# TensorE sums the gathered V rows of a mixture of experts, four tokens abreast, for two of three tiles

## The chip, the core and the metric

One Trainium2 chip, one core. The metric is the device time of one launch in microseconds (us), the median of several executions. Engines go by the names of the profile: PE is TensorE, PEld its weight loads, DVE is VectorE, ACT is ScalarE, POOL is GpSimd, SP is SyncE (it issues most DMAs); SPq, PEq and so on are their instruction queues. POOL issues the indirect (gathering) DMAs.

## The reference, cut to what matters

Two layers of a diffusion trunk over 512 latent tokens and, in layer 0, 256 context tokens of width 1024. Each layer mixes tokens (attention, a long convolution, a state space scan) and then runs a feed-forward net of 16384 experts, of which each token takes 128 (8 heads of 16):

```python
def peer_ffn(x, wq, sub_keys, u_tab, v_tab):
    ...
        best, pos = lax.top_k(cand, PEER_TOPK)
        expert = jnp.take_along_axis(cand_id, pos, axis=-1)
        gate = jax.nn.softmax(best, axis=-1)
        act = jax.nn.gelu(jnp.einsum('btd,bthkd->bthk', xc, u_tab[expert]).astype(jnp.float32))
        w = (gate * act).astype(xc.dtype)
        return jnp.einsum('bthk,bthkd->btd', w, v_tab[expert])
```

So a token's result is a sum of 128 rows of the V table, each of 1024 float32, with 128 weights. The change is in how this last sum is made for some tokens.

## The kernel before

The tokens stand in tiles of 128. There are six expert tiles to compute in layer 0 (four latent, two of context) and four in layer 1. They are computed in two ways.

*Dense* (`peer_u`, `peer_v`; four tiles in layer 0, three in layer 1): all 16384 experts for every token. `peer_u` goes through 128 chunks of the U table: DMA of 512 KB, a split into a high and a low half (ACT line 176, DVE line 160, since a product of float32 accuracy is made of three matmuls, `mm3`), 24 matmuls into the PSUM tile `pu` (layer 0, 512 columns) or `pm` (layer 1, 384 columns), GELU, and a store. `peer_v` goes through 128 steps of the V table: DMA of 512 KB (`x`, two buffers), the same split (`xh`, `xl`), the activations `va` times a gate table `gt` (loaded every eight steps), a split of that (`vwh`, `vwl`) and matmuls into accumulators `pa` that stay in PSUM for the whole loop: 24 per step in layer 0, 18 in layer 1. The gate tables come from `peer_table` (one-hot matrices `ohA`, `ohB` on DVE, matmuls into `ps`). Where the tables are done before all chunks of `peer_u` are, the chunks left over are computed inside `peer_v` ("fused" steps, into PSUM tiles `px`). In layer 1 there are such steps.

*Gathered* (`peer_gather`, lines 1191 to 1214; the two context tiles of layer 0 and one latent tile of layer 1): for each of the 128 experts of a token, one indirect DMA brings one row per token, so that a tile `gx` of 128 partitions (tokens) by 1024 floats holds the k-th expert of every token. The U phase takes 128 such tiles and DVE multiplies and sums each (line 1196). Then come GELU and the gate, and the V phase takes 128 tiles more; DVE multiplies each by the token's weight and adds it to the result (line 170, called from `add`). `gx` has four buffers: an indirect DMA waits until the tile four before it has been used.

The order of the work comes from `weave` (line 100): generators yield an estimated time and the one that is behind goes next. The framework then puts the instructions of each engine in one fixed order, by data dependencies and its own estimate of time; on the chip every engine goes through its list in order. Here the gather generator is woven with the others in three stretches: with `peer_u` and the table work (line 1531, line 1583), and then with `peer_v` (lines 1537, 1589). PSUM has eight banks. In layer 0's `peer_u` they are lent out as `m` (4), `u` (2), `s` (2); in its `peer_v` as `a` (7) and `x` (1); in layer 1 as `m` (4), `s` (2) and then `a` (6), `x` (2). `x` is needed by the fused steps.

Of the kernel before, what the change touches and what calls it, by code (L numbers as in the profile page):

```python
# [22 lines left out]
D = 1024  # L23
# [10 lines left out]
NCAND = OFFS[8] + 8  # L34
NE = 128 * 128
WAIT = -1

PV_NORM = 0
PV_GATEB = PV_NORM + NL * 2 * 8
# [7 lines left out]
class Trunk:  # L47
# [124 lines left out]
    def act(self, out, x, f, **k):  # L172
        self.nc.scalar.activation(out=out, in_=x, func=f, **k)  # L173
# [1000 lines left out]
            for x in hn:  # L1174
                self.tt(x, x, b, op)

    def gathered(self, pool, src, ids, use):

        lag, made = 1, []
        for k in range(128 + lag):  # L1180
            if k < 128:
                g = self.t(pool, [128, D], tag="gx", bufs=4)
                self.nc.gpsimd.indirect_dma_start(out=g, out_offset=None, in_=src,  # L1183
                                                  in_offset=bass.IndirectOffsetOnAxis(ap=ids[:, k:k + 1], axis=0))
                made.append(g)
            if k >= lag:
                with self.tc.issue_after(self.paced) if self.paced else nullcontext():
                    use(k - lag, made.pop(0))
            yield 1.6

    def peer_gather(self, pool, l, j, x, p, ids, dot, src, put):

        w = p[:, 2].rearrange("p h k -> p (h k)")

        def product(c, g):
            self.nc.vector.tensor_tensor_reduce(out=g, in0=g, in1=x, scale=1.0, scalar=0.0, op0=OP.mult, op1=OP.add,  # L1196
                                                accum_out=dot[:, c:c + 1])

        def add(c, g):
            if c:  # L1200
                self.stt(x, g, w[:, c:c + 1], x, OP.mult, OP.add)
            else:
                self.ts(x, g, w[:, 0:1], OP.mult)

        yield from self.gathered(pool, self.a["peer_un"], ids, product)
        self.act(dot, dot, AF.Gelu_apprx_tanh)
        self.tt(w, w, dot, OP.mult)
        yield from self.gathered(pool, self.a["peer_v"].rearrange("l e d -> (l e) d"), ids, add)
        y = self.t(pool, [128, D], tag="gx", bufs=4)
        self.nc.sync.dma_start(y, src)  # L1210
        self.tt(x, x, self.rows(pool, l, j, 5, "gx", 4), OP.mult)
        self.tt(x, x, y, OP.add)
        put(x)
        yield 4.0
# [20 lines left out]
    def peer_v(self, l, pool, h, act, G, xs, put, j):  # L1235
# [31 lines left out]
        for s in range(128):  # L1267
            i = order[s]
            if s % 8 == 0:
                gt = self.t(pool, [128, n, 8, 8, 16], tag="gt", bufs=2)  # L1270
                for q in range(n):
                    nc.sync.dma_start(gt[:, q], G[q][:, :, i:i + 8, :].rearrange("b p e t -> p b e t"))
            v = self.weights(vr[:, i:i + 1, :], None, pool, "x", 2)
            if s == 0:
                yield 0.0
            a = self.t(pool, [128, T], tag="va", bufs=2)
            if s < fused:
                u, u0 = activations(s + 1), u
                p = self.bank("x")[:, 0:T]
                for k in range(8):  # L1280
                    self.mm3(p, (u0[0][:, k], u0[1][:, k]), (h[0][:, k], h[1][:, k]), k == 0, k == 7)
                self.act(a, p, AF.Gelu_apprx_tanh)
            else:
                nc.sync.dma_start(a, act(i))
            if len(held) == 2 or held and s < 127:
                b = held.pop(0)
                for k in halves:
                    half(b, k)
            y = gt[:, :, :, i % 8, :]
            self.tt(y, a.rearrange("p (q b t) -> p q b t", q=n, b=8), y, OP.mult)  # L1290
            w = [self.t(pool, [128, n * 8, 16], F32R, tag=t, bufs=2) for t in ("vwh", "vwl")]
            with self.tc.issue_after(self.freed) if odd and 0 < s < fused else nullcontext():
                self.split(y.rearrange("p q b t -> p (q b) t"), *w)
            self.paced = self.cut.ins
            held.append((s, [z.rearrange("p b t -> p (b t)") for z in w], v))
            yield n * (2.6 if s < fused else 1.3)
        g2 = self.rows(pool, l, j, 5, "x", 2)
        for q in range(n):
            for b in held:
                for c in range(2):  # L1300
                    half(b, (q, c))
            x = self.t(self.wp, [128, D], tag="w", bufs=3)
            nc.sync.dma_start(x, xs[q])
            for c in range(2):
                k = slice(c * 512, c * 512 + 512)
                y = self.t(pool, [128, 512], tag="vy", bufs=2)
                z = acc[q, c]
                if (q, c) == odd and fused:
                    if fused < 128:
                        self.tt(part, part, z, OP.add)  # L1310
                    z = part
                self.tt(y, z, g2[:, k], OP.mult)
                self.tt(x[:, k], x[:, k], y, OP.add)
            put(q, x)
            yield 2.0

# [101 lines left out]
    def run(self):  # L1418
# [27 lines left out]
        def chain(*gens):  # L1446
            for g in gens:
                yield from g
# [69 lines left out]
        def gather():  # L1518
            for q in range(2):
                yield from until(("ids", q), "gx")  # L1520
                yield from self.peer_gather(C["gx"], 0, 1, *C[q], c1[q], lambda x: nc.sync.dma_start(c2[q], x))
            self.done.add("c2")

        side, gather = aside(), gather()
        with self.pool("ha") as ha:
            hs.append(self.halves(ha, TL))
            with self.psum(m=4, u=2, s=2), self.pool("ua") as ua:
                weave((chain(self.ctx_rest(0, xc, c1, vec[0, 0], st[0]), mark("c1"), ctx_side()), lambda: 1.1 if "c1" in self.done else 1.0, "m"),
                      (chain(until("h"), self.peer_u(0, ua, hs[0], TL, lambda i: act[i], "tabs"), mark("u")), lambda: 1.2 if "c1" in self.done else 10.0, "u"),
                      (part(side, "tables"), lambda: 1.25 if "c1" in self.done else 1.23 if "pg" in self.done else 0.8, "s"),  # L1530
                      (self.while_(gather, "tabs"), 1.69, "s"), (mods(1, range(6), 0, 1), 1.26, "m"))
            self.done.add(("mods", 1))
            with self.pool("pv", True) as pv:
                vl = self.peer_v(0, pv, hs[0], lambda i: act[i], G, x1, self.store(x2), 0)
                next(vl)
                with self.psum(a=7, x=1):
                    weave((vl, 1.0, "m"), (gather, 1.5, "s"))
# [20 lines left out]
        def gather():  # L1558
            for q in range(o):
                yield from until(("ids", 1, q))  # L1560
                yield from self.peer_gather(pg, 1, 0, hn[q], pk[q], ids[q], dot[q], x1[q], lambda x: final(q, x))

        gather = gather()
        pu = self.psum(m=4, s=2)
# [152 lines left out]
```

## Time and profile before

| | |
|---|---|
| median of 3 runs | 5661.28 us (5646.26 to 5666.2) |
| profiled execution | 5662.23 us; its span 5660.2 us |
| PE busy | 4899.3 us, 87% |
| PEld busy | 4022.5 us, 71% |
| DVE busy | 3729.2 us, 66% |
| ACT busy | 1758.3 us, 31% |
| POOL busy | 1426.1 us, 25% |
| DMA | 1333.38 MB, mean 236 GB/s |

The profile follows one execution. Its stretches, in time: token mixing of layer 0 until some 1740 us, with `peer_u` of layer 0 begun; the gathers of layer 0 begin at 1743 us; `peer_u` ends at 2543 us and `peer_v` runs until some 3400 us; token mixing of layer 1 until 4150 us; `peer_u` of layer 1 with tables until 4950 us; `peer_v` until the end. How to read it: busy shares over the whole span mix all these, so each stretch is looked at by itself. "DMA share" is the mean busy share of the core's 16 DMA engines (it can read slightly over 1), "PEclk" the granted clock of TensorE as a part of 2.4 GHz.

### The profile page before, as it was taken

Reading aid. Unit: us, or ns where it says so; the run is one execution under the profiler, and the core shown is the slowest. Engines: PE = TensorE matmul, PEld = TensorE weight load, DVE = VectorE, ACT = ScalarE, POOL = GpSimd, SP = SyncE. Lnnn points to the kernel's source line nnn. Section 1 sums busy time; section 2 is a strip of 40 time slices with the busy share of each in tenths; the row PEclk is TensorE's granted clock in tenths of the full one; section 3 lists DMA queues with packets and bytes.
Section 4 is the critical chain, followed back from the end, with each engine's and each line's share of the span. In section 5 each row is a group of like instructions: output and inputs, shape, how many; then the busy total and the mean of one; then the engine's idle time right before and its main releaser. Section 6 shows DMA issues by size and latency. Waiting matters only on the chain.

```text
span 5660.2 us, 72445 instructions
## 1 busy us (share of the span) xinstructions
PE 4899.3 (87%) x25801; PEld 4022.5 (71%) x25801; DVE 3729.2 (66%) x7594; ACT 1758.3 (31%) x2651; POOL 1426.1 (25%) x1626
## 2 busy tenths in 40 slices
PE   6798978869997888998888887998889588899898
PEld 5676657648885777786666676875678587798687
DVE  5643436644499899987676775534435989788755
ACT  3222423314432322332222223333233133333233
POOL 0003500000002343433444440405000322254400
PEclk7899989889998999999998998998999899999999
DMA  6557335666556888899999986561545777799975
GB/s 207 190 185 263 106 117 183 201 205 185 176 179 207 306 291 314 319 325 343 319 317 311 320 307 205 166 224 58 157 157 168 242 252 243 256 338 333 333 239 176
DMA packets 641793, 1333.38 MB, mean 236 GB/s; under 512 B 56437, under 2 KB 342390, under 8 KB 626328
## 3 DMA queue, kind: packets, MB, share of 16 engines
q1 hardware_dynamic: 522776, 871.53, 47.1%
q0 software_dynamic: 118656, 457.23, 23.0%
q8 instruction: 203, 3.33, 0.2%
q14 instruction: 158, 1.29, 0.1%
HBM read 1147.01 MB, written 181.49 MB: 235 GB/s over the span
## 4 chain that ended last, share of the span: by engine, by line
PE 27%; DVE 12%; DMA 11%; issue 10%; POOL 4%; ACT 1%; SPq 1%; POOLq 0%; DVEq 0%; ACTq 0%
PE pa L181 9%; PE two L181 4%; PE ps L181 4%; PE pu L181 3%; POOL gx L1183 3%; PE px L181 2%; DMA va<-t 2%; PE pf L181 2%; DMA gx<-in_peer_v_dram,t 2%; DVE t L170 2%; DVE wl L160 2%; PE pm L181 2%; DMA gx<-in_peer_un_dram,t 1%; DVE gx L1196 1%; DMA t<-ge 1%
## 5 line engine op out<-in xcount | busy, mean ns | idle before, releaser
L176 ACT CAST wh<-w 128x1024 fp32r<-128x1024 f32 (+1 forms) x550 | 545.9, 993 | 1611.2 <-PE pu L181 395.3
L160 DVE TENSOR_TENSOR wl<-w,wh 128x1024 fp32r<-128x1024 f32 (+1 forms) x550 | 639.4, 1164 | 555.4 <-ACT wh L176 545.3
L1183 POOL DMA_INDIRECT gx<-in_peer_un_dram,t x384 | 527.9, 1375 | 1501.1 <-DVE t L1196 691.6
L181 PE MATMUL pa<-xl,vwh 128*128 128x512 f32 x1664 | 673.1, 405 | 124.1 <-DVE xl L160 123.7
L1183 POOL DMA_INDIRECT gx<-in_peer_v_dram,t x384 | 543.6, 1416 | 680.1 <-DVE t L170 579.9
L181 PE MATMUL pa<-xh,vwh 128*128 128x512 f32 x1664 | 665.8, 401 | 28.1 <-ACT xh L176 21.4
L181 PE MATMUL pu<-t,wh 128*128 128x512 f32 x2048 | 659.0, 403 | 28.5 <-ACT ua L173 20.7
L181 PE MATMUL pa<-xh,vwl 128*128 128x512 f32 x1664 | 665.1, 400 | 1.2 <-DVE ss L167 1.1
L181 PE MATMUL pm<-t,wh 128*128 128x384 f32 (+1 forms) x2432 | 586.0, 328 | 59.1 <-ACT wh L176 54.4
L170 DVE SCALAR_TENSOR_TENSOR t<-gx,t,t 128x1024 f32<-128x1024 f32 x381 | 488.4, 1282 | 35.2 <-DMA gx<-in_peer_v_dram,t 33.3
L1196 DVE CUSTOM_DVE_ANT_0 gx<-gx,t 128x1024 f32<-128x1024 f32 x384 | 465.3, 1220 | 57.8 <-DMA gx<-in_peer_un_dram,t 57.4
L181 PEld LDWEIGHTS pm<-t,wh 128*128 128x128 f32 x2432 | 431.1, 196 | 77.7 <-ACT wh L176 72.2
L181 PEld LDWEIGHTS pa<-xl,vwh 128*128 128x128 f32 x1664 | 323.0, 194 | 213.2 <-DVE xl L160 147.0
L181 PEld LDWEIGHTS pu<-t,wh 128*128 128x128 f32 x2048 | 389.6, 194 | 111.6 <-ACT ua L173 26.8
L181 PE MATMUL pu<-t,wl 128*128 128x512 f32 x1024 | 412.9, 404 | 60.4 <-DVE wl L160 60.4
L181 PE MATMUL pm<-t,wl 128*128 128x384 f32 (+1 forms) x1216 | 396.9, 329 | 49.1 <-DVE wl L160 49.0
L181 PEld LDWEIGHTS pa<-xh,vwh 128*128 128x128 f32 x1664 | 322.0, 194 | 103.6 <-ACT xh L176 27.7
L176 ACT CAST vwh<-gt 128x512 fp32r<-128x512 f32 (+1 forms) x256 | 145.3, 568 | 794.9 <-PE pa L181 671.2
L181 PEld LDWEIGHTS pa<-xh,vwl 128*128 128x128 f32 x1664 | 323.5, 194 | 70.8 <-DVE vwl L160 3.5
L176 ACT CAST xh<-x 128x1024 fp32r<-128x1024 f32 x256 | 268.2, 1048 | 252.4 <-DMA x<-in_peer_v_dram 208.0
L160 DVE TENSOR_TENSOR xl<-x,xh 128x1024 fp32r<-128x1024 f32 x256 | 312.7, 1221 | 26.2 <-ACT xh L176 25.8
L160 DVE TENSOR_TENSOR gt<-va,gt 128x512 f32<-128x512 f32 (+1 forms) x256 | 156.6, 622 | 262.2 <-DMA va<-t 107.9
(371 smaller groups left out, 9154.3 us busy)
## 6 DMA issues: line engine op xcount, KB each, us to landing
w<-in_peer_u_dram SPq DMA_DIRECT2D x256, 512.0 KB
x<-in_peer_v_dram SPq DMA_DIRECT2D x256, 512.0 KB
w<-in_in_w_dram SPq DMA_DIRECT2D x128, 512.0 KB
t<-ge SPq DMA_DIRECT2D x56, 1024.0 KB
gt<-t SPq DMA_DIRECT2D x112, 512.0 KB
w<-in_mod_w_dram SPq DMA_DIRECT2D x96, 512.0 KB
dft<-in_dft_dram POOLq DMA_DIRECT2D x32, 1024.0 KB, 6.8
t<-ua SPq DMA_DIRECT2D x128, 256.0 KB
```

Source lines behind the costliest of these rows:

```text
L160: return (e or self.nc.vector).tensor_tensor(out=out, in0=a, in1=b, op=op)
L170: self.nc.vector.scalar_tensor_tensor(out=out, in0=a, scalar=s, in1=b, op0=op0, op1=op1)
L176: self.nc.scalar.copy(h, x)
L181: self.nc.tensor.matmul(out, l, r, start=start, stop=stop)
L1183: self.nc.gpsimd.indirect_dma_start(out=g, out_offset=None, in_=src, in_offset=bass.IndirectOffsetOnAxis(ap=ids[:, k:k + 1], axis=0))
L1196: self.nc.vector.tensor_tensor_reduce(out=g, in0=g, in1=x, scale=1.0, scalar=0.0, op0=OP.mult, op1=OP.add, accum_out=dot[:, c:c + 1])
```

## The change

For the first context tile of layer 0 and for the gathered tile of layer 1 the V phase is done by TensorE (new function `summed`). The indices and weights are transposed, so that one indirect DMA now brings the 128 rows of *one token* onto 128 partitions. A matmul with the 128 weights as one column among 32 (the others zero) as its stationary operand sums them. Four tokens, whose columns are in the four groups of 32 columns of the array, make a group: eight matmuls of 512 columns, four into each of two PSUM accumulators, 32 groups in all. The accumulators are taken from lane `m` in layer 0 and from `x` in layer 1; so the phase waits until the modulation matmuls (`("mods", 1)`) or the fused steps (`("fused", 1)`) are done. The second context tile keeps DVE. The buffers of `gx` become 7 in layer 0 and 8 in layer 1, for all gathers; in `peer_v` the tile `vy` is dropped (its product is written in place).

```diff
-    def gathered(self, pool, src, ids, use):
+    def gathered(self, pool, l, src, ids, use):
...
-                g = self.t(pool, [128, D], tag="gx", bufs=4)
+                g = self.t(pool, [128, D], tag="gx", bufs=GX[l])     # GX = [7, 8]
...
+    def summed(self, pool, l, src, ids, w, lane):
+        nc = self.nc
+        p = self.bank(lane)
+        f = self.t(pool, [128, 128], tag="gi", bufs=1)
+        nc.vector.tensor_copy(f, ids)
+        nc.tensor.transpose(p[:, 0:128], f, self.ident)
+        nc.tensor.transpose(p[:, 128:256], w, self.ident)
+        it = self.t(pool, [128, 128], I32, tag="git", bufs=1)
+        nc.vector.tensor_copy(it, p[:, 0:128])
+        wt = self.t(pool, [128, 4, 32], tag="gi", bufs=1)
+        nc.vector.tensor_copy(wt.rearrange("p g s -> p (g s)"), p[:, 128:256])
+        acc = [self.bank(lane) for _ in range(2)]
+        lag, made = GX[l] - 4, []
+        for n in range(128 + lag):
+            if n < 128:
+                t = 32 * (n % 4) + n // 4
+                g = self.t(pool, [128, D], tag="gx", bufs=GX[l])
+                nc.gpsimd.indirect_dma_start(out=g, out_offset=None, in_=src,
+                                             in_offset=bass.IndirectOffsetOnAxis(ap=it[:, t:t + 1], axis=0))
+                made.append(g)
+            if n % 4 == (lag - 1) % 4:
+                s = (n - lag - 3) // 4
+                if s >= 0:
+                    if s % 4 == 0:
+                        z = self.t(pool, [128, 4, 4, 32], tag="gz", bufs=2)
+                        nc.vector.memset(z, 0.0)
+                        nc.vector.tensor_copy(z.rearrange("p g s c -> p g (s c)")[:, :, s:s + 100:33], wt[:, :, s:s + 4])
+                    rows = [made.pop(0) for _ in range(4)]
+                    for c in range(2):
+                        for q in range(4):
+                            self.mm(acc[c][32 * q:32 * q + 32, :], z[:, q, s % 4, :], rows[q][:, c * 512:(c + 1) * 512], s == 0, s == 31)
+                yield 6.4
+        return acc
...
+        if lane:
+            yield from self.until(*[key] * (key is not None))
+            acc = yield from self.summed(pool, l, rows, ids, w, lane)
+        else:
+            yield from self.gathered(pool, l, rows, ids, add)
...
-                yield from self.peer_gather(C["gx"], 0, 1, *C[q], c1[q], lambda x: nc.sync.dma_start(c2[q], x))
+                yield from self.peer_gather(C["gx"], 0, 1, *C[q], c1[q], lambda x: nc.sync.dma_start(c2[q], x),
+                                            None if q else "m", ("mods", 1))
...
-                yield from self.peer_gather(pg, 1, 0, hn[q], pk[q], ids[q], dot[q], x1[q], lambda x: final(q, x))
+                yield from self.peer_gather(pg, 1, 0, hn[q], pk[q], ids[q], dot[q], x1[q], lambda x: final(q, x), "x", ("fused", 1))
```

Three places in the program's order (no times are in it). The first is TensorE's list in layer 0 where `peer_u` (`pu`) ends and `peer_v` (`pa`) begins, of the kernel before:

```order
L181 MATMUL pu_21586<-t_7724,wh_21581 128x512
L181 MATMUL pu_21586<-t_7723,wl_21582 128x512
L181 MATMUL pu_21586<-t_7723,wh_21581 128x512
L181 MATMUL pu_21586<-t_7724,wh_21581 128x512
L181 MATMUL pu_21586<-t_7723,wl_21582 128x512
L181 MATMUL pa_21658<-xh_21626,vwh_21637 128x512
L181 MATMUL pa_21662<-xh_21626,vwh_21637 128x512
```

And of the change, the last rows of 56 that stand there between the last `pu` and the first `pa` (`gx` is a token's gathered rows, `gz` the weight columns, `pm` the two accumulators):

```order
L182 MATMUL pm_18681<-gx_22199,gz_22017 32x512
L182 MATMUL pm_18682<-gx_22199,gz_22017 32x512
L182 MATMUL pm_18681<-gx_22201,gz_22017 32x512
L182 MATMUL pm_18682<-gx_22201,gz_22017 32x512
L182 MATMUL pm_18681<-gx_22203,gz_22017 32x512
L182 MATMUL pm_18682<-gx_22203,gz_22017 32x512
L182 MATMUL pm_18681<-gx_22287,gz_22017 32x512
L182 MATMUL pm_18682<-gx_22287,gz_22017 32x512
L182 MATMUL pa_21792<-xh_21753,vwh_21764 128x512
L182 MATMUL pa_21792<-xl_21754,vwh_21764 128x512
```

What moved: between the last `pu` and the first `pa` there was nothing; now the last seven of the 32 groups (28 tokens) stand there, since `peer_v` needs the PSUM banks that they accumulate in. The other 25 groups stand between chunks of `pu`, most of them two chunks apart, six of them one chunk. The second place is TensorE's list there, one such group among the chunks, of the change (`ps` is table work):

```order
L182 MATMUL ps_20107<-ohB_20054,ohA_20053 128x128 x4
L182 MATMUL pm_18681<-gx_19991,gz_20121 32x512
L182 MATMUL pm_18681<-gx_19993,gz_20121 32x512
L182 MATMUL pm_18681<-gx_19995,gz_20121 32x512
L182 MATMUL pm_18681<-gx_20113,gz_20121 32x512
L182 MATMUL pm_18682<-gx_19991,gz_20121 32x512
L182 MATMUL pm_18682<-gx_19993,gz_20121 32x512
L182 MATMUL pm_18682<-gx_19995,gz_20121 32x512
L182 MATMUL pm_18682<-gx_20113,gz_20121 32x512
L182 MATMUL ps_20139<-ohB_20101,ohA_20100 128x128 x4
```

What moved: DVE's four operations on four tiles `gx` became these eight matmuls. The third place is the start of layer 1's V phase. Before, on DVE, it began in a fused step of `peer_v` (`wl` and `w` are the U table's chunk of such a step):

```order
L160 TENSOR_TENSOR t_33412<-t_33412,t_33414 128x128
L165 TENSOR_SCALAR t_33411<-gx_40446,t_33412 128x1024
L160 TENSOR_TENSOR wl_40606<-w_40604,wh_40605 128x1024
L160 TENSOR_TENSOR gt_39956<-va_40457,gt_39956 128x24x16
L160 TENSOR_TENSOR vwl_40510<-gt_39956,vwh_40509 128x384
L170 SCALAR_TENSOR_TENSOR t_33411<-gx_40448,t_33412,t_33411 128x1024
```

Now it begins on TensorE after 34 of the 128 steps of `peer_v`, all fused steps being done (`px` are the accumulators):

```order
L182 MATMUL pa_40236<-xh_42214,vwl_42241 128x512
L182 MATMUL px_42203<-gx_42205,gz_42283 32x512
L182 MATMUL px_42203<-gx_42207,gz_42283 32x512
L182 MATMUL px_42203<-gx_42209,gz_42283 32x512
L182 MATMUL px_42203<-gx_42211,gz_42283 32x512
L182 MATMUL px_42204<-gx_42205,gz_42283 32x512
L182 MATMUL px_42204<-gx_42207,gz_42283 32x512
L182 MATMUL px_42204<-gx_42209,gz_42283 32x512
L182 MATMUL px_42204<-gx_42211,gz_42283 32x512
L182 MATMUL pa_40216<-xh_42245,vwh_42271 128x512
```

What moved: the 32 groups stand over 82 steps of `peer_v` that have no U chunk, two or three steps apart, and 12 steps follow the last; before, the V phase of this tile began at the fourth step.

## Rows read from the trace of the kernel before

**Rows 1.** Busy us by stretch: PE, PEld, DVE, ACT, POOL; PEclk; DMA share; GB/s.

```profile
1740.00:2180.00 440.00, 364.28 (x1747) 302.12 (x1746) 400.49 (x1090) 120.09 (x177) 177.19 (x132) 0.92 0.83 290
2180.00:2543.00 363.00, 339.53 (x1713) 286.61 (x1712) 325.98 (x699) 111.86 (x166) 144.04 (x103) 0.98 0.88 314
2549.00:2640.00 91.00, 82.71 (x333) 65.63 (x333) 72.37 (x82) 22.34 (x28) 35.45 (x27) 0.94 1.01 350
2640.00:3400.00 760.00, 646.82 (x2667) 519.12 (x2667) 550.75 (x698) 177.51 (x223) 337.54 (x242) 0.91 0.92 316
4350.00:4950.00 600.00, 470.05 (x2690) 448.04 (x2689) 519.40 (x1482) 180.63 (x271) 154.61 (x112) 0.90 0.72 247
4950.00:5200.00 250.00, 249.61 (x1264) 226.35 (x1263) 212.39 (x236) 87.56 (x120) 134.68 (x93) 1.00 0.93 334
5200.00:5400.00 200.00, 174.38 (x690) 136.19 (x690) 154.12 (x183) 59.28 (x80) 77.08 (x52) 0.93 0.96 328
5400.00:5600.00 200.00, 199.33 (x879) 164.45 (x878) 110.89 (x150) 72.03 (x97) 0.00 (x0) 1.00 0.74 227
```

**Rows 2.** Chain that ended last, end of layer 0's peer_u: start us, us, what.

```profile
2432.88 1.78 PE ps L181 x16
2434.67 5.46 PE pu L181 x24
...
2527.09 16.35 PE pu L181 x72
...
2548.70 5.10 PE pa L181 x12
```

**Rows 3.** The same chain, the last 260 us.

```profile
5420.90 220.04 PE pa L181 x967
```

**Rows 4.** PE in order of time, stationary x columns: matmuls of 32 columns among others.

```profile
1056.55 0.28 PE L181 MATMUL pm<-t,wl 128*128 128x256 f32 x1
1056.76 1.07 PE L181 MATMUL pm<-w,t 128*32 128x256 f32 x16
1057.76 0.50 PE L181 MATMUL pm<-t,wh 128*128 128x256 f32 x2
...
1184.94 0.64 PE L181 MATMUL pm<-w,t 128*32 128x256 f32 x8
1185.40 1.89 PE L181 MATMUL pm<-t,t 128*32 128x256 f32 x8
```

**Rows 5.** Operations on gx, whole span: count, ns min/median/max.

```profile
L1183 POOL DMA_INDIRECT gx<-in_peer_v_dram,t x384: 939/1486/3090, 2170.8 to 5368.9; - x192
L170 DVE SCALAR_TENSOR_TENSOR t<-gx,t,t x381: 1257/1280/1331, 2181.3 to 5381.4; 128x1024 f32<-128x1024 f32 x191
...
DMA to landing us min/median/max: 4.1/7.3/11.2
```

**Rows 6.** Waits of PE, 2180 to 2543 us: us in total, times, longest.

```profile
PE ps L181 <- DVE ohA L167: 8.2, 4, 7.1
PE pu L181 <- DVE wl L160: 7.9, 6, 2.2
```

**Rows 7.** Waits of DVE, 1740 to 2180 us.

```profile
DVE gx L1196 <- DMA gx<-in_peer_un_dram,t: 23.1, 21, 4.1
```

**Rows 8.** Waits of DVE, 4350 to 4950 us.

```profile
DVE gx L1196 <- DMA gx<-in_peer_un_dram,t: 16.0, 7, 8.1
```

**Rows 9.** Waits of DVE, 2640 to 3400 us.

```profile
DVE gt L160 <- DMA gt<-t: 94.3, 9, 12.0
```

**Rows 10.** What POOL sat idle for before its gathers, 2640 to 3400 us.

```profile
DVE t L1196: 218.4, 111
DVE t L170: 186.4, 100
```

**Rows 11.** Busy us around one wait for gt, columns as in Rows 1.

```profile
3095.00:3100.00 5.00, 4.18 (x18) 2.98 (x16) 0.49 (x1) 1.51 (x2) 0.94 (x1) 1.00 1.09 358
3100.00:3105.00 5.00, 0.09 (x1) 0.00 (x0) 0.30 (x1) 0.06 (x1) 0.00 (x0) 0.78 0.66 236
3105.00:3110.00 5.00, 2.82 (x7) 2.25 (x8) 5.00 (x6) 1.04 (x1) 1.15 (x1) 0.50 0.46 157
```

**Rows 12.** Groups by line and shape, PE: count, busy us, mean ns, idle before.

```profile
L181 PE MATMUL px<-t,wh 128*128 128x384 f32 x512 | 130.5, 336 | 0.0
```

More of the change, by code (lines that the diff above doesn't have):

```diff
@@ L36 @@
 WAIT = -1
+GX = [7, 8]
 PV_NORM = 0
@@ L1189, in gathered, with peer_gather @@
             yield 1.6
-    def peer_gather(self, pool, l, j, x, p, ids, dot, src, put):
+    def summed(self, pool, l, src, ids, w, lane):
[31 more added lines that the diff above has]
+        return acc
+    def peer_gather(self, pool, l, j, x, p, ids, dot, src, put, lane=None, key=None):
         w = p[:, 2].rearrange("p h k -> p (h k)")
@@ L1203, in add @@
                 self.ts(x, g, w[:, 0:1], OP.mult)
-        yield from self.gathered(pool, self.a["peer_un"], ids, product)
+        yield from self.gathered(pool, l, self.a["peer_un"], ids, product)
         self.act(dot, dot, AF.Gelu_apprx_tanh)
         self.tt(w, w, dot, OP.mult)
-        yield from self.gathered(pool, self.a["peer_v"].rearrange("l e d -> (l e) d"), ids, add)
-        y = self.t(pool, [128, D], tag="gx", bufs=4)
+        rows = self.a["peer_v"].rearrange("l e d -> (l e) d")
+        if lane:
[3 more added lines that the diff above has]
+            yield from self.gathered(pool, l, rows, ids, add)
+        y = self.t(pool, [128, D], tag="gx", bufs=GX[l])
         self.nc.sync.dma_start(y, src)
-        self.tt(x, x, self.rows(pool, l, j, 5, "gx", 4), OP.mult)
+        r = self.rows(pool, l, j, 5, "gx", GX[l])
+        for c in range(2):
+            k = slice(c * 512, c * 512 + 512)
+            self.tt(x[:, k], acc[c] if lane else x[:, k], r[:, k], OP.mult)
         self.tt(x, x, y, OP.add)
@@ L1283, in peer_v @@
             else:
+                self.done.add(("fused", l))
                 nc.sync.dma_start(a, act(i))
@@ L1305, in peer_v @@
                 k = slice(c * 512, c * 512 + 512)
-                y = self.t(pool, [128, 512], tag="vy", bufs=2)
                 z = acc[q, c]
@@ L1311, in peer_v @@
                     z = part
-                self.tt(y, z, g2[:, k], OP.mult)
-                self.tt(x[:, k], x[:, k], y, OP.add)
+                self.tt(z, z, g2[:, k], OP.mult)
+                self.tt(x[:, k], x[:, k], z, OP.add)
             put(q, x)
@@ L1530, in run @@
                       (part(side, "tables"), lambda: 1.25 if "c1" in self.done else 1.23 if "pg" in self.done else 0.8, "s"),
-                      (self.while_(gather, "tabs"), 1.69, "s"), (mods(1, range(6), 0, 1), 1.26, "m"))
-            self.done.add(("mods", 1))
+                      (self.while_(gather, "tabs"), 1.69, "s"), (chain(mods(1, range(6), 0, 1), mark(("mods", 1))), 1.26, "m"))
             with self.pool("pv", True) as pv:
```

## The prediction

> **What bounds the kernel now.** I read the busy times by stretch first [rows 1], then the chain that ended last in the stretches where the gathers run [rows 2, 3], then the waits. The reader should see that "DVE 66%" says nothing here; each stretch has its own bound. From 1740 to 2180 us (U phase of layer 0's first gathered tile, with table work) DVE is busy 400 of 440 us and PE waits. From 2180 to 2543 (its V phase) PE is busy 339.5 of 363, and in the second half of that stretch the chain is nothing but PE: 5.46 us of a `peer_u` chunk, 1.78 us of table matmuls, again and again [rows 2]. From 2549 to 3400 the DMA share is 1.01, then 0.92, PE 85 to 91%: transfers and the eight-step wait for `gt` (94.3 us in 9 waits [rows 9]) bound it. In layer 1, 4350 to 4950 is DVE's (519 of 600). In 4950 to 5200, the fused steps, PE is full (249.6 of 250) although 93 gathers run beside it. In 5200 to 5400 the DMA share is 0.96 and PE falls to 174 of 200; after the gathers have ended PE is full again with a DMA share of 0.74, and the chain is one piece of 967 matmuls of 0.2275 us [rows 3].
>
> So in the V phases of both changed tiles PE is the bound or close to it, and DVE, which is relieved, is not.
>
> **The change part by part.** All sums are against the profiled execution, 5662.23 us with a span of 5660.2; the median of the runs is 5661.28, 1 us less, which I neglect.
>
> *Taken from DVE:* 127 multiply-adds of 1.28 us per tile [rows 5], 163 us, twice. What it is worth is only what PE waits for DVE: in 2180 to 2543 that is 8.2 + 7.9 = 16.1 us [rows 6]; in layer 1 it is inside the 25.6 us that PE idles in 5200 to 5400, counted below.
>
> *Added to PE:* a group of four tokens is eight matmuls of 512 columns. The nearest rows are four matmuls of 32 stationary and 256 moving columns that sit in the four column groups; float32 takes two rows each. Eight rows last 0.64 us and sixteen 1.07 [rows 4], so each further four matmuls take 0.43 us at 256 columns, 0.86 at 512, and two halves 1.72. Between the start of the sixteen and the next full-width matmul lies 1.00 us [rows 4], 0.14 over their own 0.86, and 0.09 or so before: with 0.23 for both a group costs 1.95 us, 62 us for 32 groups. The Trainium skill, "TensorEngine Tiling (Array Packing)", Key Properties, says that changing the tiling mode drains TensorE, which speaks against a group that is set alone between full-width matmuls; it gives no price. The row has that drain in it (0.23 us, 13 us over the 58 places). If each switch instead cost a whole 0.28 us matmul, it would be 32 us, 19 more. The small DVE work for the columns (eight clears and copies per tile, three copies for the transposes) is tens of us at most, on an engine that was given 163.
>
> *Layer 0, chunks of `peer_u`:* 25 groups stand there: 25 x 1.95 = 49 us, less the 16 us of waits for DVE that go. With seven buffers the last tile of a group is issued only when the group before it has run; it is there 1.5 us (POOL) + 7.3 us (landing) later [rows 5]. Two chunks apart (14.5 us) that is covered; the six groups one chunk apart (7.24 us) wait some 1.5 us each, 9 in all. Together +42; between +25 (no wait, all PE idleness of this stretch gone) and +60.
>
> *Layer 0, hand-over:* seven groups stand between the last `pu` and the first `pa`, with nothing else for PE to do. Their first 107 tiles can be on the way; the other 21 gathers follow one another at POOL's 1.49 us: 31 us, the last lands 7.3 us later, 2 us for sums and read-out: 40 us, where PE used to start `peer_v` 5.3 us after `peer_u` [rows 2]. That is +35. In return the first steps of `peer_v` have no V gathers beside them: 2549 to 2640 holds 333 matmuls, 13.9 steps, 76 us at 5.46, and took 91 [rows 1]; I give back 10 of these 15. Net +25; between +4 (21 x 0.94 us and 4.1 us to land [rows 5], all 15 back) and +80 (six rounds of issue, 11.2 us to land, and sums).
>
> *Deeper buffers:* U phases: DVE's waits for gathered rows, 23.1 and 16.0 us [rows 7, 8]; DVE is the bound there, yet part of what it gains it waits again elsewhere: -8 each, from 0 to all. In 2640 to 3400 POOL idles 405 us for buffers [rows 10] and DMA falls to half just after each `gt` wait [rows 11]. Three more gathers could run in that wait. But the dip comes when all buffers are full and the consumers have just restarted; that happens with seven too, and until then the gathers compete with the very `gt` that is awaited. I take -12, from -61 (760 x 0.08, DMA full all the time [rows 1]) to +20.
>
> *Layer 1, fused steps:* 512 matmuls of one kind, 16 per step, are 32 fused steps [rows 12]. PE is full there before; gathers and DVE work taken away give nothing.
>
> *Layer 1, the other 96 steps:* before, 96 x 18 x 0.2275 = 393 us plus 25.6 idle in 5200 to 5400: 418. Now 82 of them hold all 128 gathers, 1.56 per step. DMA time: a step alone takes 4.095 us x 0.74 = 3.03 us of all engines [rows 1, 3]; 5200 to 5400 holds 690/18 = 38.3 steps and 52 gathers in 192 us of DMA, so a gather takes (192 - 116)/52 = 1.46. A step then needs 3.03 + 1.56 x 1.46 = 5.3 us of DMA, against 4.095 + 0.76 = 4.86 of PE. So DMA bounds it: 82 x 5.25 = 430, with 14 steps at 4.095 = 57: 487, +69. Not less than PE's own 336 + 62 + 57 = 455, +37; with the DMA share of 0.96 as in 5200 to 5400, 5.5 us per step, +90. The tile's end lies 12 steps, 49 us, before `peer_v`'s, so its read-out hides.
>
> Sum: +42 + 25 - 8 - 8 - 12 + 69 = +108: 5770 us.
>
> **Rivals.**
>
> *PE waits for rows in its own list everywhere:* an engine in order cannot go past a late gather, DVE's lateness cost less. Layer 1 at +90, chunks at +60, hand-over at +60, buffers -20: +190, 5852 us. For it: landings of up to 11.2 us and DMA near 1. Against: eight buffers in layer 1 give two groups of lead.
>
> *Faster, by the buffers:* in 2640 to 3400 the idle POOL was what let DMA drop to 0.92; seven buffers fill it and the stretch ends near 700 us. -61 there, -39 in the U phases, +25, +4 and +37 elsewhere: -34, 5628 us. It decides if that stretch runs with a DMA share of 1.0. For it: POOL's 405 us of idleness. Against: 350 GB/s and share 1.01 were reached only beside the start of `peer_v`, and PE is the bound in between. The Trainium skill, "DMA: Bandwidth & Descriptors", SWDGE vs HWDGE vs iDMA, has each DMA engine take turns between the queues of the two kinds; by that, more gathers outstanding take bandwidth from `gt`. The trace agrees in that `gt` comes late just where gathers run; by it alone this rival falls and the term is nearer +20.
>
> *The change doesn't do what it says, the four are not abreast:* eight rows that don't overlap last 1.89 us, 0.22 each [rows 4], twice that at 512 columns: 6.9 us per group instead of 1.95, 64 x 5 = 317 us more, 6087 us. The order speaks against it (the four column groups alternate), save for the last seven groups.
>
> *It evens out:* buffers at -50, layer 1 at +37, hand-over +4, chunks +25: +16, near 5670.
>
> **How the numbers follow.** Forecast 0.63 (own range 5710 to 5810), PE waiting everywhere 0.17, faster 0.11, not abreast 0.03, evened out 0.06. Range 5690 to 5850: it holds the forecast and most of the first rival. 0.3% is 17 us, about what a measurement of this kernel tells from none. Faster 0.12, same 0.06, slower 0.82.
>
> **What would show it.** Right: PE idle for some 40 us between the last `pu` and the first `pa` in layer 0, matmuls of 32 columns only; a group takes about 2 us; steps of layer 1 with gathers take 5.2 to 5.5 us at a DMA share near 1; the fused steps take as long as before. Wrong: no such gap, the 2640 to 3400 stretch much shorter, PE still full beside the gathers of layer 1.

## The result, and the profile after

The changed kernel takes 5843.3 us (median of 4 runs, 5838.2 to 5847.0), the kernel before beside it 5653.8: ratio 1.033, interval 1.0308 to 1.0352. The forecast of 5770 had the sign, but the loss is 181 us against the 5662 us from which the sum was made, not 108. The time lies outside the forecast's own range (5710 to 5810), and inside the whole range (5690 to 5850) by 7 us, since that range was drawn to hold most of the first rival. The profiled execution has a span of 5836.4 us.

First the busy times by stretch of the changed kernel, cut at its own events; columns as in [rows 1].

```profile
1740.00:2190.00 450.00, 391.60 (x1861) 323.90 (x1860) 410.99 (x1155) 126.71 (x185) 174.93 (x129) 0.94 0.83 292
2190.00:2561.00 371.00, 368.12 (x2031) 277.55 (x2029) 198.52 (x536) 107.52 (x159) 111.26 (x105) 1.00 0.84 294
2561.00:2639.00 78.00, 39.47 (x115) 9.09 (x114) 13.47 (x19) 3.92 (x5) 25.48 (x27) 0.77 0.92 320
2639.00:3488.00 849.00, 737.43 (x3072) 597.33 (x3071) 593.19 (x753) 201.36 (x253) 347.92 (x248) 0.92 0.88 301
4440.00:5004.00 564.00, 444.02 (x2568) 421.58 (x2567) 500.40 (x1461) 170.33 (x257) 159.96 (x116) 0.91 0.74 254
5004.00:5276.00 272.00, 267.19 (x1349) 241.24 (x1348) 134.48 (x173) 96.23 (x132) 19.18 (x12) 1.00 0.59 188
5276.00:5476.00 200.00, 172.54 (x782) 121.53 (x781) 79.06 (x115) 48.29 (x65) 57.99 (x56) 0.93 0.86 299
5476.00:5676.00 200.00, 175.66 (x831) 123.91 (x830) 81.83 (x115) 52.91 (x70) 57.17 (x52) 0.95 0.87 304
```

Against [rows 1]: VectorE is relieved where it should be (198.5 of 371 us in the V phase of layer 0, 326.0 of 363 before), and TensorE is now full there. Two places are new. From 2561 to 2639 TensorE is half idle, and from 5276 on neither TensorE (0.87) nor the DMA engines (0.86) are full, though the forecast had the DMA engines bound this last stretch.

To compare kernels I cut each trace at the same seven events: layer 0's first gather, the last `pu`, the first and last `pa` of layer 0's `peer_v`, the first and last matmul of the fused steps (`px` from a U chunk), the last `pa`. Stretches in us; the forecast column is the prediction's sum, put on the same cuts.

| stretch | before | forecast | after | change |
|---|---|---|---|---|
| first gather to last `pu` | 800.0 | +34 | 824.2 | +24 |
| last `pu` to first `pa` (hand-over) | 5.3 | +35 | 77.4 | +72 |
| layer 0's `peer_v` | 867.6 | -22 | 848.9 | -19 |
| from there to the fused steps (layer 1's U phase in it) | 1526.2 | -8 | 1515.9 | -10 |
| fused steps | 258.1 | 0 | 263.4 | +5 |
| layer 1's `peer_v` after them | 445.4 | +69 | 555.2 | +110 |

With 6 us less ahead of the first gather these make +176, the difference of the two spans. Two rows miss: the hand-over by 37 us and the end of layer 1 by 41. The expectations below still end the fused steps at the two transposes of layer 1's sum, 8 us behind the last fused matmul: their 547 us is 555 here, and their 14 + 101 is 5 + 110.

**The hand-over.** TensorE of the changed kernel, in order of time: start, us, operation; in brackets the idle time before it and what ended it.

```profile
2561.26 3.63 PE L182 MATMUL pm<-gx,gz 128*32 128x512 f32 x28
2568.70 2.74 PE L182 MATMUL pm<-gx,gz 128*32 128x512 f32 x4 [3.81 <-DMA gx<-in_peer_v_dram,git]
2572.73 21.84 PE L182 MATMUL pm<-gx,gz 128*32 128x512 f32 x56 [1.28 <-DMA gx<-in_peer_v_dram,git]
...
2599.68 6.92 PE L182 MATMUL pm<-gx,gz 128*32 128x512 f32 x16 [0.58 <-DMA gx<-in_peer_v_dram,git]
2638.74 0.77 PE L182 MATMUL pa<-xh,vwh 128*128 128x512 f32 x1 [32.13 <-DVE t L161]
```

The sums end 45 us after the last `pu` (2606.6), close to the 40 forecast. Then TensorE stands still for 32.13 us, until VectorE has read the accumulators out. VectorE, same kernel:

```profile
2605.97 0.69 DVE L161 TENSOR_TENSOR gt<-va,gt 128x512 f32<-128x512 f32 x1 [59.76 <-DMA va<-t]
...
2635.54 0.69 DVE L161 TENSOR_TENSOR gt<-va,gt 128x512 f32<-128x512 f32 x1 [1.95 <-DMA va<-t]
2637.31 1.29 DVE L161 TENSOR_TENSOR t<-pm,gx 128x512 f32<-128x512 f32 x2 [1.08 <-DMA gx<-t]
```

Between the first and the last product `gt<-va,gt` of these stand ten more, each waiting for its `va`; the read-out `t<-pm,gx` stands behind all twelve. But its own last wait is for `gx<-t`, the row that it multiplies by. And the first product waits 59.76 us: its `va` is asked for late, at 2584.7 us, and is there some 21 us after that. SyncE's list, the kernel before and then the changed one:

```profile
2533.25 0.32 SPq L1231 DMA_DIRECT2D t<-ua  x1
2533.62 3.58 SPq L1272 DMA_DIRECT2D gt<-t  x3
...
2544.13 0.32 SPq L1231 DMA_DIRECT2D t<-ua  x1
```

```profile
2551.16 11.20 SPq L1276 DMA_DIRECT2D t<-ua  x3
2564.05 11.05 SPq L1317 DMA_DIRECT2D gt<-t  x4
2575.15 9.55 SPq L193 DMA_DIRECT2D x<-in_peer_v_dram  x1
2584.74 1.28 SPq L1330 DMA_DIRECT2D va<-t  x1
...
2632.13 0.32 SPq L247 DMA_DIRECT2D gx<-t  x1
```

Before, `peer_v`'s first `gt` was issued ahead of the last stores of `peer_u`'s results; now behind all of them, 3 us after the last `pu`, and each issue takes longer (11.05 us for four, 3.58 for three before). The read-out's row (`gx<-t`) is asked for at 2632.13, behind twelve loads of `va` in the same list, some 25 us after the sums are done. So with its loads in this order and no product ahead of it, the read-out would have started about 1 us earlier: two late orders hold it at once, VectorE's and SyncE's.

**Layer 1 after the fused steps.** VectorE, ScalarE and TensorE of the changed kernel around one of seven stalls of 5.5 us or more:

```profile
5371.72 1.23 DVE L161 TENSOR_TENSOR xl<-x,xh 128x1024 fp32r<-128x1024 f32 x1 [0.39 <-ACT xh L177]
5384.82 1.03 DVE L161 TENSOR_TENSOR gt<-va,gt 128x384 f32<-128x384 f32 x2 [11.87 <-DMA gt<-t]
5385.76 0.55 DVE L161 TENSOR_TENSOR vwl<-gt,vwh 128x384 fp32r<-128x384 f32 x1
5386.23 1.22 DVE L161 TENSOR_TENSOR xl<-x,xh 128x1024 fp32r<-128x1024 f32 x1
...
5377.82 1.05 ACT L177 CAST xh<-x 128x1024 fp32r<-128x1024 f32 x1 [0.88 <-DMA x<-in_peer_v_dram]
...
5387.50 0.79 PE L182 MATMUL pa<-xl,vwh 128*128 128x512 f32 x1 [6.58 <-DVE xl L161]
```

`xh` is there at 5378.9, so `xl`, 1.22 us of work, could have been done at 5380.1. It is done at 5387.4, because two products of the *next* `gt` stand in front of it in VectorE's list and wait for that load. TensorE needs those products seven steps later and `xl` now. The gathered rows themselves are hardly ever late: TensorE waits 2.5 us for them in this whole stretch and 55.9 us for `xl`.

After each of the seven TensorE runs at the lower of its two clock levels (granted clock 0.50) for 3.5 us or more. Windows of the changed kernel, columns as above:

```profile
5575.60:5580.10 4.50, 4.46 (x11) 3.50 (x12) 1.58 (x2) 0.00 (x0) 0.00 (x0) 0.50 0.78 236
5583.60:5591.80 8.20, 8.20 (x40) 6.69 (x37) 3.34 (x5) 1.46 (x2) 4.06 (x4) 1.00 0.75 267
```

A stall of 6.21 us ended at 5575.6; the next 4.5 us have a granted clock of 0.50 and hold 11 matmuls where 20 would go at 0.2275 us: 2 us more per stall.

### The profile page after: what moved, and what is told of

It is laid out like the page before. It is cut to its first block, busy times and chain, and to the rows that moved or that the text cites. A ratio compares the mean times of both kernels' runs of the same rounds, so it can differ in the third digit from the quotient of the medians.

```text
span 5836.4 us, 73926 instructions
## 1 busy us (share of the span) xinstructions
PE 5058.2 (87%) x26829; PEld 4057.1 (70%) x26829; DVE 3442.2 (59%) x7379; ACT 1760.4 (30%) x2651; POOL 1335.0 (23%) x1626
## 4 chain that ended last, share of the span: by engine, by line
PE 30%; DMA 13%; issue 8%; DVE 8%; ACT 1%; POOL 1%; SPq 1%; DVEq 0%; ACTq 0%; POOLq 0%
PE pa L182 12%; PE pu L182 4%; DMA va<-t 4%; DMA gt<-t 4%; PE px L182 3%; PE two L182 3%; PE ps L182 3%; PE pm L182 2%; PE pf L182 2%; DMA t<-ge 2%; DVE gx L1233 1%; DVE xl L161 1%; DMA w<-in_peer_u_dram 1%; DVE wl L161 1%; DMA x<-in_peer_v_dram 1%
## 5 line engine op out<-in xcount | busy, mean ns | idle before, releaser
L1211 POOL DMA_INDIRECT gx<-in_peer_v_dram,git x256 | 268.4, 1049 | 872.7 <-PE px L182 303.1
L182 PE MATMUL ps<-ohB,ohA 128*128 128x128 f32 x1792 | 248.5, 288 | 43.0 <-ACT ge L1142 33.6
```

Of the source, the lines that this page charges most:

```text
L182: self.nc.tensor.matmul(out, l, r, start=start, stop=stop)
```

## The experiments

Twelve runs; medians of four runs each (ten for e11), ratio to the kernel before with its interval, and the stretches of the table above.

| run | us | ratio | to last `pu` | hand-over | L0 `peer_v` | between | fused | L1 after |
|---|---|---|---|---|---|---|---|---|
| after | 5843 | 1.033 (1.031-1.035) | 824 | 77 | 849 | 1516 | 263 | 555 |
| e1 | 5605 | 0.990 (0.988-0.992) | 788 | 5 | 861 | 1498 | 264 | 446 |
| e2 | 5710 | 1.009 (1.008-1.011) | 826 | 77 | 849 | 1507 | 265 | 441 |
| e3 | 5722 | 1.010 (1.007-1.014) | 785 | 5 | 859 | 1509 | 264 | 559 |
| e4 | 5822 | 1.028 (1.025-1.030) | 823 | 48 | 875 | 1529 | 263 | 559 |
| e5 | 5775 | 1.023 (1.019-1.026) | 858 | 16 | 856 | 1484 | 264 | 551 |
| e6 | 5764 | 1.021 (1.018-1.024) | 824 | 77 | 843 | 1507 | 265 | 495 |
| e7 | 5811 | 1.028 (1.025-1.031) | 831 | 77 | 849 | 1529 | 263 | 528 |
| e9 | 5839 | 1.033 (1.029-1.036) | 824 | 78 | 847 | 1516 | 268 | 560 |
| e10 | 5775 | 1.020 (1.017-1.023) | 826 | 78 | 847 | 1518 | 263 | 505 |
| e11 | 5678 | 1.004 (1.002-1.006) | 879 | 16 | 790 | 1492 | 271 | 493 |
| e12 | 5714 | 1.011 (1.008-1.014) | 835 | 68 | 783 | 1512 | 266 | 497 |
| e8 | 5549 | 0.981 (0.978-0.984) | 790 | 16 | 802 | 1500 | 264 | 439 |

The column "between" varies from 1484 to 1529 among kernels that hardly differ there; I have no cause for it, and read no total finer than some 20 us for that reason. The other stretches repeat within some 8 us where kernels agree.

**The parts (e1, e2, e3).** Edits: the V sum goes back to VectorE in both tiles (e1), in layer 1's alone (e2), in layer 0's alone (e3); the deep buffers stay.

```
e1, e3  - None if q else "m", ("mods", 1))
        + None)
e1, e2  - lambda x: final(q, x), "x", ("fused", 1))
        + lambda x: final(q, x))
```

> Deeper buffers alone (seven and eight), both V phases on VectorE as before. Theory: the buffers gave back what the changed kernel's trace shows outside the V phases: 6 us before the first gather, about 8 in layer 0's U phase, 13 in layer 1's, and some of the 19 by which peer_v of layer 0 became shorter, while the whole loss is the sums on TensorE. Then this is 20 to 40 us faster than before (ratio 0.993 to 0.996). Rival: the deeper buffers are themselves the cost in layer 1 (more gathers outstanding make gt late): then the 96 other steps of layer 1 take well over 445 us here too, towards 500, and the time is 30 to 60 us above before.

> TensorE sums layer 0's tile only; layer 1's tile is VectorE's again, buffers deep. Theory (costs add, each tile pays in its own stretch): the 14 + 101 us of layer 1 go, the 24 + 72 us of layer 0 stay; 115 us less than the changed kernel, about 5730, ratio to before 1.010 to 1.018. Rival (what layer 1 loses is DMA work that its stretch lacks in any case): little goes, over 5790.

> TensorE sums layer 1's tile only; layer 0's tile is VectorE's again, buffers deep. Theory (costs add): the gap of 77 us between peer_u and peer_v falls to about 5, and the chunks' 30 us go: about 100 less than the changed kernel, 5740, ratio to before 1.012 to 1.020; the steps of layer 1 stay at 545 to 550 us. Rival: with V rows gathered beside the start of peer_v again, peer_v takes 20 to 30 us more and only 70 are won, 5770.

e1 wins 1.0% (0.8 to 1.2), more than expected: the buffers, with the change's small edits outside the sums (`vy`), are a gain of 53 us, and all of the loss is the sums. e2 has the changed kernel's layer 0 and e1's layer 1, e3 the reverse, stretch by stretch: the costs add, 105 us for layer 0's tile and 117 for layer 1's over e1. Both totals lie some 20 us under the theory's, as e1's own does. e1's rival is out (446 us in layer 1), and so are e2's (over 5790) and e3's: `peer_v` is 859 us, 10 more than the changed kernel's and not 20 to 30, and the time is 5722, not 5770.

**The hand-over (e4, e5).** e4 lets ScalarE copy the sums out of PSUM at once; e5 ends the sum earlier by a lower weight of its chain.

```
e4  + for c in range(2):
    +     self.nc.scalar.copy(x[:, c * 512:c * 512 + 512], acc[c])
    - self.tt(x[:, k], acc[c] if lane else x[:, k], r[:, k], OP.mult)
    + self.tt(x[:, k], x[:, k], r[:, k], OP.mult)
e5  + self.done.add("vsum")
    ...
    - (self.while_(gather, "tabs"), 1.69, "s")
    + (self.while_(gather, "tabs"), lambda: 1.2 if "vsum" in self.done else 1.69, "s")
```

> The changed kernel, but ScalarE copies the two summed accumulators out of PSUM as soon as they are done, and VectorE then works on the copy. Theory: the second half of the hand-over (32 us of idle TensorE) is that the read-out stands in VectorE's list behind a dozen gt products that wait for their loads, while peer_v's first accumulator needs the freed banks: the gap falls from 77 to some 45 to 50 us, 5815, ratio to the changed kernel about 0.995. Rival: peer_v could not have begun earlier anyway, since its own v rows and gt products come only then: the gap stays within 5 us of 77, the time within 0.2 % of the changed kernel's.

> The changed kernel, but once layer 0's V sum has begun its chain gets the weight 1.2 in place of 1.69, so that all 32 groups stand among the chunks of peer_u and none behind them. Theory (the 77 us between the last pu and the first pa are TensorE waiting for the last gathers and then for a read-out behind other work): the gap falls to about 5 to 10 us, the stretch up to the last pu grows by 7 groups and some waits for rows, 824 to 840-850; peer_v, which gained 12 us by the empty start, gives that back. Together 35 to 55 less than the changed kernel. Rival (as in the run with ScalarE's read-out, an earlier peer_v only waits for its loads): the gap goes, but peer_v grows by 45 to 60 and the time stays within 10 us of the changed kernel's.

e4's gap fell as the theory said, to 48 us, and the gain was lost: `peer_v` took 26 us longer, so up to its end e4 won 5 us. TensorE in e4:

```profile
2600.64 0.50 PE L182 MATMUL pa<-xh,vwh 128*128 128x512 f32 x1 [0.68 <-ACT t L1250]
...
2635.46 0.80 PE L182 MATMUL pa<-xl,vwh 128*128 128x512 f32 x1 [23.38 <-DVE xl L161]
```

It does two steps and then waits for `xl`, which stands behind the same late products in VectorE's list. Only the name of the wait changed. e4 says nothing of the row `gx<-t`, since its copy needs none. In e5 the gap is 16 us, but the chunks grew by 33, more than forecast; up to `peer_v`'s end 21 us are won. The rest of its total comes out of "between", and I don't count it.

**What bounds layer 1 (e6, e7, e9, e10).** e6 halves the bytes of a gather, e7 TensorE's matmuls per group; e9 asks for `gt` four steps earlier (`gates` makes the tile and loads it); e10 gives the product a tile of its own.

```
e6  + if l:
    +     self.ts(f, f, 2.0, OP.mult)
    +     src = src.rearrange("e (h d) -> (e h) d", h=2)
    ...
    + h = D // 2 if l else D
    - out=g, out_offset=None, in_=src,
    + out=g[:, :h], out_offset=None, in_=src,
    ...
    - rows[q][:, c * 512:(c + 1) * 512]
    + rows[q][:, c * (0 if l else 512):c * (0 if l else 512) + 512]
e7  ...
    - for c in range(2):
    + for c in range(1 if l else 2):
    ...
e9  ...
    + if s % 8 == 3 and s < 120:
    +     nxt = gates(s + 8 - s % 8)
e10 - self.tt(y, a.rearrange("p (q b t) -> p q b t", q=n, b=8), y, OP.mult)
    + z = self.t(pool, [128, n, 8, 16], tag="vy", bufs=2) if l else y
    + self.tt(z, a.rearrange("p (q b t) -> p q b t", q=n, b=8), y, OP.mult)
    + y = z
```

> In layer 1 each gather of the V rows brings 512 columns (half a row) in place of 1024; both halves of the sum multiply these same 512 columns, so TensorE's work is unchanged and the result is not the reference's. Theory A (the DMA engines' time sets the steps with gathers, as the prediction had it): the 128 gathers need some 90 us less of DMA time and the 547 us after the fused steps fall by 60 or more, to 455-485. Theory B (loads that are late for their latency and their order of issue, at a DMA share near 0.83): a fall of 10 to 40. Theory C (TensorE's own work): none, within 8 us.

> In layer 1 TensorE multiplies only the first 512 columns of the gathered V rows, four matmuls per group in place of eight; the read-out uses that half twice, so the result is not the reference's. The gathers are unchanged. Theory C (TensorE's work adds to the steps, at 1.9 us a group): 32 groups at about half, 28 to 32 us less after the fused steps, 515 to 520. Theory A (DMA sets the steps): no change, within 8 us. Theory B (late loads, with stalls at fixed places): 28 to 32 less too, if the loads don't just come as late; less than 15 if they do.

> The changed kernel, but the gate tiles gt of the next eight steps of peer_v are loaded after the fourth of the eight before them in place of with the step that needs them first (two buffers, as before). Theory B: what stops TensorE every eight steps is that gt's load is issued by the step that waits for it; with it early the gt waits (120 us in layer 0's peer_v, 70 in layer 1's) go, TensorE's 92 and 58 us of waits fall to less than half, and the time is 50 to 90 us less than the changed kernel's. Theory A (the DMA engines are the bound there): the same bytes have to come, the waits move to va and x, and less than 20 us is won.

> The changed kernel, but in layer 1 the products of peer_v go to a tile of their own (two buffers) in place of back into gt. In the changed kernel's trace gt's next load waits for the last reader of products that lie in gt, up to eight steps later, and in VectorE's list two products of the next gt, seven steps ahead of TensorE, stand in front of the vwl and xl that TensorE needs next. Theory B (these products hold VectorE until gt has landed, and TensorE with it): the gt waits (70 us) and most of TensorE's 56 us of waits and of its half-clock stretches behind them go; the 547 us after the fused steps become 480 to 510. Theory A (DMA bound, late loads would only move): less than 15 us.

e7 won 27 us: TensorE's share comes on top, it hides nowhere (theory C; 28 to 32 were expected, and theory B allowed as much). e6 won 60 us, by the expectation's numbers theory A, the DMA engines as the bound. But the changed kernel's DMA share there is 0.86, and e10, with every byte in place, won 50. That fits bytes that matter by making loads late: in e6 VectorE's waits for `gt` fall from 70 to 37 us. TensorE's waits after the fused steps (us in total, times, longest), in the changed kernel, in e6 and in e10:

```profile
PE pa L182 <- DVE xl L161: 55.9, 15, 7.0
PE px L182 <- DMA gx<-in_peer_v_dram,git: 2.5, 3, 1.1
```

```profile
PE pa L182 <- DVE xl L161: 15.0, 5, 3.8
```

```profile
PE pa L182 <- ACT xh L177: 9.4, 8, 4.6
PE pa L182 <- DVE xl L161: 5.8, 8, 0.8
```

And the same windows of the three as busy times:

```profile
5276.00:5740.00 464.00, 405.64 (x1870) 286.07 (x1872) 182.16 (x257) 116.67 (x157) 131.38 (x124) 0.94 0.85 296
```

```profile
5276.00:5660.00 384.00, 368.90 (x1778) 262.90 (x1778) 172.99 (x239) 108.37 (x148) 120.27 (x112) 0.98 0.78 256
```

```profile
5276.00:5690.00 414.00, 390.32 (x1881) 275.11 (x1880) 180.30 (x243) 116.28 (x155) 127.40 (x122) 0.99 0.94 332
```

In e10 a product goes to a tile of which there are two, so products stay two to four steps ahead of TensorE (seven in the stall above), and `gt` is free as soon as it is multiplied. No run tells these two effects of the edit apart. TensorE's waits shrink to 15 us, its clock is 0.99, and only now are the DMA engines nearly full. e9 tested nothing: in SyncE's list the loads of `gt` stand where they stood in the changed kernel, so its null result says nothing on lateness.

The Trainium skill, "Perfetto Trace Analysis", Optimization Strategy, says that the same gap repeating on the engine that should be saturated can mean that there isn't room for the next tile. The trace agrees: the gap came every eight steps (5387.5, 5435.4 us), and a tile of two buffers took it away (55.9 us to 15).

**Both faults mended (e11, e12), and VectorE's sums with the same tile (e8).** e11 is e5 with product tiles in both layers, e12 the changed kernel with them, e8 is e1 with them. For the space, e11 and e12 have six buffers in layer 0.

```
e11, e12  - GX = [7, 8]
          + GX = [6, 8]
all       + z = self.t(pool, [128, n, 8, 16], tag="vy", bufs=2)
          + self.tt(z, a.rearrange("p (q b t) -> p q b t", q=n, b=8), y, OP.mult)
          + y = z
```

> The changed kernel with its two faults mended: layer 0's sum ends among the chunks of peer_u (weight 1.2, as in the run before), and both layers' products of peer_v have a tile of their own; layer 0's gathered tiles get six buffers in place of seven, for the space. Theory: 60 to 70 from the hand-over, 40 to 65 from layer 1, 30 to 80 from the gt stalls in layer 0's peer_v: 5640 to 5710. What is left against the run without sums on TensorE and with the same tiles is then TensorE's own 32 groups per tile, about 62 us twice. Rival: DMA is the bound in both peer_v stretches; only the hand-over's part comes, 5760 to 5780.

> Sums on VectorE as before, buffers deep (seven and eight), and the products of peer_v in tiles of their own in both layers. Theory B: the stall of every eight steps goes in layer 0's peer_v too, where TensorE waited 99 us for xl: 40 to 90 less than with the deep buffers alone, ratio to before 0.975 to 0.985; TensorE's sums are then no help anywhere. Rival (DMA share 0.92 to 0.95 is the bound of that stretch): less than 20 won, ratio 0.987 to 0.991.

> The changed kernel with product tiles of their own in peer_v of both layers and six buffers for layer 0's gathered tiles, but its seven last groups still behind peer_u: the run before it, without the earlier end of the sum. In VectorE's list four products now stand between the last work for peer_u and the read-out, two of them with buffers that are free at once, in place of twelve. Theory (the second half of the gap is VectorE's list, the first the last gathers): the gap falls from 77 to 45 to 55 us, peer_v takes 790 to 810 us (no growth as with ScalarE's read-out, since xl stands no longer behind products either), and the time is 5665 to 5700, that is within 20 us of the kernel with the earlier end of the sum, since seven groups cost about the same there among the chunks. Rival (the read-out waits for its own rows and for loads, whatever stands ahead): the gap stays above 70 and the time is 5705 to 5730.

e8 beats both kernels: ratio 0.981 (0.978 to 0.984), 5549 us. Against e1 it wins 58 us in layer 0's `peer_v`, and loses 11 of them in a longer hand-over. TensorE's largest wait there, in e1 and in e8:

```profile
PE pa L182 <- DVE xl L161: 99.2, 23, 7.5
```

```profile
PE pa L182 <- ACT xh L177: 41.6, 21, 4.7
```

and the busy times of the two:

```profile
2530.00:3391.00 861.00, 740.67 (x3072) 597.44 (x3072) 636.69 (x798) 204.82 (x257) 385.86 (x274) 0.92 0.93 322
```

```profile
2530.00:3320.00 790.00, 728.63 (x3027) 583.96 (x3026) 623.53 (x782) 201.95 (x254) 371.67 (x271) 0.96 0.99 346
```

So the stall of every eight steps was in the kernel before too ([rows 9, 11]); it isn't the change's, only dearer with it in layer 1. e8 against e11 is the change without the stalls and most of the gap: 128 us dearer (1.004 against 0.981), inside what was expected of both. 64 groups at the 1.94 us shown in the next section are 124. That the two agree so well is in part luck: in e11 TensorE also waits 15 us for rows, with its six buffers, and "between" is 7 us shorter.

e12's read-out no longer stands behind twelve products, yet the gap stays at 68 us, nearer to the rival than to the 45 to 55 expected, and the time of 5714 is the rival's too. VectorE in e12:

```profile
2613.13 0.69 DVE L161 TENSOR_TENSOR vy<-va,gt 128x512 f32<-128x512 f32 x1 [57.56 <-DMA va<-t]
...
2637.23 1.29 DVE L161 TENSOR_TENSOR t<-pm,gx 128x512 f32<-128x512 f32 x2 [8.32 <-DMA gx<-t]
```

Loads that SyncE issues late end both waits: the read-out's row is asked for at 2630.9 us here too. So the theory's second half was wrong: the products alone don't hold the gap. From the first gather to `peer_v`'s end e12 takes 1686 us and e11 1685: where the last seven groups stand makes no difference there. The 36 us between the two totals (32 in the profiled executions) lie elsewhere, 20 in "between" and 12 ahead of the first gather.

## Why the prediction was right in sign and short in size

- **A group costs 1.95 us: right.** TensorE in e10, where nothing is late; the last matmul of a step starts at 5409.19 and its successor would at 5409.42:

```profile
5409.19 0.39 PE L182 MATMUL pa<-xh,vwl 128*128 128x512 f32 x1
5409.51 1.92 PE L182 MATMUL px<-gx,gz 128*32 128x512 f32 x16
5411.36 0.50 PE L182 MATMUL pa<-xh,vwh 128*128 128x512 f32 x1
```

  5411.36 - 5409.42 = 1.94, and 31 of e10's 32 groups take the same. The drain at a change of tiling mode that the prediction took from the Trainium skill, "TensorEngine Tiling (Array Packing)", Key Properties, is within the 0.22 us over the 1.72 of the matmuls' own, as [rows 4] had it.
- **Chunks of `peer_u`, +42: right.** Against e1, which has the same buffers, +37 (824 against 788). TensorE waits 2.7 us there for gathered rows, 9 were allowed.
- **Hand-over, net +25: wrong.** It is 72 us of gap less the 12 by which `peer_v` is shorter than e1's, +60, inside the bounds of 4 and 80. The step that failed is "2 us for sums and read-out": TensorE waited 32 us for the read-out, which stands behind twelve products in VectorE's list and whose own row SyncE asks for 25 us after the sums; SyncE issues all these loads behind `peer_u`'s last stores. e4 shows that the wait is the read-out's, e12 that the products alone don't make it; that SyncE's order does is read from the traces and not tested. The 10 us given back were right (12). I had looked at TensorE's list and at POOL's, not at the order in VectorE's and SyncE's. And shortening the gap alone wins little (e4): VectorE's list is late for `xl` as well.
- **Deeper buffers, -28: too small.** e1 measured -53: 14 in layer 0's U phase (427 to 413 us from the first U gather to the first V gather), 23 in layer 1's (621 to 598; 8 were taken for each), 7 in `peer_v` (12 taken). There VectorE's waits for `gt` grew, from 94 us to 117.
- **Fused steps, 0: right.** 263.4 us against e1's 263.7; once they run, both kernels do 255 matmuls in 50 us.
- **Layer 1 after the fused steps, +69: wrong, and so was its argument.** It was +110, and a step with gathers took 5.96 us, not 5.2 to 5.5. "So DMA bounds it" failed: with a share of 0.86 it didn't. Two things add where the prediction took the larger of PE's work and the DMA's: TensorE's own 62 us (e10 has 66 over e8), and 50 us of stalls by VectorE's list (the changed kernel over e10), which the prediction had at nothing. With VectorE's sums that list cost little there (e8 wins 7 us over e1), with 46 gathers in the stretch; with 128 it cost 50. The forecast, 445 + 69 = 514 us on this cut, is nearly what e10 takes: 505, with 5.35 us per step at a share of 0.94. That step is 0.49 us over TensorE's own 4.86, so the DMA engines may count in e10; no run tells.
- **The rivals.** "PE waits for rows in its own list everywhere" gave 5852 us, near the 5843 measured, but by another mechanism: TensorE waits 2.7 us for rows in the chunks, 6.3 in the hand-over and 2.5 in layer 1. That the range held the time is owed to this rival, so it is luck. "Not abreast" fell by the group's 1.94 us. "Faster, by the buffers" priced a gain in `peer_v` that the depth didn't bring; the product's tile brought it (861 to 802 in e8, DMA share 0.99). The +20 that the prediction set against it did not come either (e1's -7). And its reading that `gt` comes late just where gathers run holds in layer 0 alone: in layer 1 of the kernel before, VectorE's waits from 4950 to 5385 us, beside the gathers, hold none for `gt`, and those after the gathers hold six of up to 2.3 us.

The sum has two slips that change little: 82 steps of 5.3 us are 435, not 430, and +16 is 5678, not 5670.

Left open: why "between" varies by 45 us (the changed kernel has 18 more there than e1, which no term above explains); what the hand-over would cost if SyncE issued `peer_v`'s first loads and the read-out's row ahead of the last stores; and which of the two effects of the product's tile counts. No run tests any of this.

## What to carry to other kernels

Work moved onto the engine that is full in that stretch costs its whole duration, here 64 x 1.94 us, whatever the share of the relieved engine. When a wait's releaser is a short instruction, read what stands ahead of it in that engine's list: an instruction put there early for a later step can hold it, and a result written back into a loaded tile keeps that tile's buffer until the last reader. Take such run-ahead away (a small tile of its own, two buffers) before an engine is blamed. Then look at what the instruction itself waits for: here, in the hand-over, its own load was as late as those ahead of it, and clearing the list ahead (e12) left the gap.

## What was not expected of the hardware

- In layer 1's `peer_v` the same bytes moved at a DMA share of 0.85 in the changed kernel and of 0.94 in e10, where only the products have a tile of their own; in layer 0's at 0.93 (e1) and 0.99 (e8).
- The deeper gather buffers (e1) are worth 1.0% (0.8 to 1.2), most of it in the U phases, where VectorE waited only 16 to 23 us for gathered rows.
- A stall of 6.21 us costs about 2 us more, at a granted clock of 0.50 for 4.5 us behind it; the clock is 0.50 behind each of the seven.
